# Diagonal products on TensorE for the sum of layer 0's experts, and two groups of layer 1's adaLN products at other places

## The chip, the cores and the metric

The kernel runs on one core of a Trainium2 chip. The core has five engines with a queue each: TensorE (PE; its weight loads are listed as PEld), VectorE (DVE), ScalarE (ACT), GpSimd (POOL) and SyncE (SP), which here only issues DMAs. Each engine takes its instructions in the order of its queue and waits on semaphores for the others. The metric is the device time of the kernel in microseconds, median of the runs.

## The reference

Two layers of a diffusion backbone over 512 tokens of 1024 features: 256 context tokens and 256 latent ones. Every layer computes six modulation vectors from the conditioning, mixes tokens in three branches and then sends each token to two of 16 experts:

```python
m = modulation(c, w_ada, b_ada)          # silu(c) @ w_ada + b_ada, split in 6 x 1024
mc = modulation(c_ctx, w_ada, b_ada)
h = concat(modulate(rms_norm(ctx, norm1), mc[0], mc[1]), modulate(rms_norm(x, norm1), m[0], m[1]))
mix = token_mixers(h, ...)               # neighbourhood attention, HGRN2, window attention
x = x + m[2] * mix                       # and ctx with mc
hx = modulate(rms_norm(x, norm2), m[3], m[4])
y = moe_ffn(hx, w_router, b_router, w_gate, w_up, w_down)
x = x + m[5] * y                         # and ctx with mc, in layer 0
```

In `moe_ffn` each token has two experts and two weights that sum to 1; an expert is `(silu(h @ w_gate) * (h @ w_up)) @ w_down`, and `y` is the weighted sum of a token's two rows.

## The kernel before, in words

Large products run as three passes of fp32r with the operands split into a high and a low half (`mm3`, L242 to L245). ScalarE casts the high half of a weight piece (`whi`, L231), VectorE subtracts it for the low one (`wlo`, L232). Weight pieces of 1 MB (`wraw`) come over SP's queue (L215) into a ring of slots, `wst`; in layer 0's tail it has twelve, of the tags raw, praw, mg and qraw. A slot is free when its piece has been read for the last time, by VectorE for a piece that is split, by TensorE for one that is not. SP issues in order, so a load whose slot is not free holds the later ones. A scheduler places the instructions of each queue.

**adaLN.** `ada_group(l, g)` (L252) makes 2048 columns, two of the six modulation vectors, of layer l: eight pieces of `w_ada` (L260), with each four f32 products of 32x512 that stand side by side in the array's columns (L262), 32 products in one bank, psd; then VectorE adds the bias (L266) and four DMAs on ScalarE's queue write the result to `m_dram` (L268). A product leaves two records in the trace, so a piece leaves eight. Five groups run inside layer 0's mixers, piece by piece between weight pieces of the projection (`ada_step` out of `split_piece`): (0,1), (0,2), (1,0), (1,1), (1,2). The last two hold layer 1's vectors 2 to 5, which are read first in layer 1's tail.

**Mixers.** The projection of layer 0's tokens, `psg<-hTh,whi` and its two companions, goes on between the mixers' own products. The HGRN mixer is a chain of VectorE, ScalarE, GpSimd and TensorE steps over chunks (L482 to L566) that ends in `yb`, written by VectorE at L566, and TensorE then multiplies yb by its projection.

**Router.** After the output projection each of four tiles of 128 tokens is transposed (L1098), multiplied by the router (L1106) and written to `h2d` (L1113). `route` works on two tiles at a time in small VectorE steps, TensorE counts ranks (L1273, L1274, L1283) and places tokens with one-hot masks M (VectorE L1309, TensorE L1313, 16 products for each tile). From the result come the gather indices `gix` (L1334). A branch on the largest expert count (`cnt`, L1148) follows on all engines. While this runs, `fetch` loads the first twelve pieces of expert weights into the twelve slots.

**Experts.** Each of the 16 gathers 128 rows (L1371, on GpSimd's queue), transposes them (L1402), multiplies by gate and up (4 pieces) and, one expert later, by down (2 pieces), and scatters the rows to `yd` (L1376). The pieces go out in the order in which they are used. The last two experts do not scatter: their rows stay on chip (`spare`, split in two fp32r halves) and a matrix MT carries them back to the tokens (`back_matrix`, L1447).

**Sum.** `combine` (L1636) loads the two rows y0, y1 of each token in `yd` (L1648), and for each tile of 128 tokens ScalarE scales them by the token's weights `wts` (L1654, L1655), GpSimd and VectorE add them, multiply by the modulation m5 and add to x, on 384 and 640 columns (L1656 to L1660). For the two experts on chip TensorE multiplies `spare` by MT, four products a half-tile (L1667), VectorE multiplies by m5 into `tm` (L1669) and adds to x (L1670). Tiles 0 and 1 are the context, 2 and 3 the latents; behind x follow layer 1's norm (L304, L307), the transposes (L395) and its first products, `psg<-whi,hTh`.

## Time and profile before

| | us |
|---|---|
| median of 3 runs | 1770.28 (1768.99 to 1772.41) |
| the profiled execution | 1766.91 |
| its span in the trace | 1764.8 |
| TensorE busy | 1653.8 (94%) |
| VectorE busy | 1049.4 (59%) |
| ScalarE busy | 818.7 (46%) |
| GpSimd busy | 346.2 (20%) |

The times in the rows are microseconds from the span's start. Of the 1766.91 us of the profiled execution 2.1 lie outside the span. An engine's share over the whole span does not say what limits a stage: for that the table by stretch is read, then the rows of the engine that waits there, with what ended its wait in brackets.

### The profile page before, as it was taken

Reading aid. Unit: us, or ns where it says so; the run is one execution under the profiler, and the core shown is the slowest. Engines: PE = TensorE matmul, PEld = TensorE weight load, DVE = VectorE, ACT = ScalarE, POOL = GpSimd, SP = SyncE. Lnnn points to the kernel's source line nnn. Section 1 sums busy time; section 2 is a strip of 40 time slices with the busy share of each in tenths; the row PEclk is TensorE's granted clock in tenths of the full one; section 3 lists DMA queues with packets and bytes.
Section 4 is the critical chain, followed back from the end, with each engine's and each line's share of the span. In section 5 each row is a group of like instructions: output and inputs, shape, how many; then the busy total and the mean of one; then the engine's idle time right before and its main releaser. Section 6 shows DMA issues by size and latency. Waiting matters only on the chain. (4 is left out here: it accounts for less than half of the span.)

```text
span 1764.8 us, 24182 instructions
## 1 busy us (share of the span) xinstructions
PE 1653.8 (94%) x8912; PEld 1218.6 (69%) x8913; DVE 1049.4 (59%) x1908; ACT 818.7 (46%) x1353; POOL 346.2 (20%) x343
## 2 busy tenths in 40 slices
PE   8999999999999999589999996999999999699998
PEld 4657677887677788477877774878887888443333
DVE  4328482447867335688888889488548786411101
ACT  3313232336676442368778774444446875301100
POOL 0003040222300123411221104143213202100000
PEclk9999999999999999799999997999999999899999
DMA  9895747523211355499999962322524345899996
GB/s 289 295 321 175 245 168 257 183 73 96 60 49 36 101 183 196 170 315 368 369 328 364 363 237 86 113 79 60 191 82 105 105 120 204 342 413 414 412 378 269
DMA packets 235312, 380.02 MB, mean 215 GB/s; under 512 B 33447, under 2 KB 130215, under 8 KB 225585
## 3 DMA queue, kind: packets, MB, share of 16 engines
q1 hardware_dynamic: 223248, 361.19, 59.1%
q10 hardware_dynamic: 7616, 9.43, 1.6%
q0 software_dynamic: 4320, 7.75, 1.3%
q8 instruction: 74, 1.21, 0.3%
q14 instruction: 54, 0.43, 0.1%
HBM read 370.50 MB, written 17.72 MB: 220 GB/s over the span
## 5 line engine op out<-in xcount | busy, mean ns | idle before, releaser
L232 DVE TENSOR_TENSOR wlo<-wraw,whi 128x1024 fp32r<-128x1024 f32 (+2 forms) x368 | 438.6, 1212 | 176.1 <-ACT whi L231 161.6
L231 ACT CAST whi<-wraw 128x1024 fp32r<-128x1024 f32 (+2 forms) x368 | 369.4, 1023 | 171.1 <-PE psg L245 77.2
L243 PE MATMUL psg<-hTh,whi 128*128 128x512 f32 (+1 forms) x576 | 206.6, 360 | 0.0
L244 PE MATMUL psg<-hTl,whi 128*128 128x512 f32 (+1 forms) x576 | 205.4, 357 | 0.0
L245 PE MATMUL psg<-hTh,wlo 128*128 128x512 f32 (+1 forms) x576 | 204.2, 356 | 0.0
L243 PE MATMUL psg<-whi,hTh 128*128 128x512 f32 (+1 forms) x392 | 148.6, 383 | 2.2 <-ACT hTh L373 2.1
L244 PE MATMUL psg<-wlo,hTh 128*128 128x512 f32 (+1 forms) x392 | 148.1, 379 | 0.0
L245 PE MATMUL psg<-whi,hTl 128*128 128x512 f32 (+1 forms) x392 | 147.3, 379 | 0.5 <-DVE hTl L404 0.4
L243 PEld LDWEIGHTS psg<-hTh,whi 128*128 128x128 f32 x576 | 109.1, 190 | 27.1 <-issue 10.1
L245 PEld LDWEIGHTS psg<-hTh,wlo 128*128 128x128 f32 x576 | 109.0, 190 | 19.0 <-issue 6.1
L244 PEld LDWEIGHTS psg<-hTl,whi 128*128 128x128 f32 x576 | 109.3, 190 | 16.0 <-issue 4.0
L1478 PE MATMUL psg<-wraw,xT 128*64 128x512 f32 x512 | 113.2, 595 | 2.9 <-PEq L1149 2.7
L243 PE MATMUL psg<-whi,xh 128*128 128x512 f32 x256 | 101.8, 398 | 0.7 <-ACT xh L1403 0.7
L244 PE MATMUL psg<-wlo,xh 128*128 128x512 f32 x256 | 100.0, 391 | 0.0
L245 PE MATMUL psg<-whi,xl 128*128 128x512 f32 x256 | 99.6, 390 | 0.0
L243 PEld LDWEIGHTS psg<-whi,hTh 128*128 128x128 f32 x392 | 74.3, 190 | 19.5 <-ACT hTh L373 3.8
L1478 PEld LDWEIGHTS psg<-wraw,xT 128*64 128x64 f32 x512 | 35.9, 137 | 74.4 <-issue 72.2
L245 PEld LDWEIGHTS psg<-whi,hTl 128*128 128x128 f32 x392 | 73.9, 189 | 16.8 <-DVE hTl L404 1.7
L244 PEld LDWEIGHTS psg<-wlo,hTh 128*128 128x128 f32 x392 | 74.4, 190 | 13.3 <-issue 0.5
L587 ACT ACTIVATE P<-P,smx 128x512 f32<-128x512 f32 (+1 forms) x96 | 62.2, 648 | 22.9 <-DVE smx L586 20.4
L836 POOL TENSOR_TENSOR mg<-mg,gates 128x512 f32<-128x512 f32 (+1 forms) x32 | 38.1, 1198 | 172.1 <-DVE gates L835 126.2
L1371 POOL DMA_INDIRECT xg<-h2d,gix x16 | 27.8, 1739 | 204.5 <-PE pst L1402 188.5
(414 smaller groups left out, 3256.9 us busy)
## 6 DMA issues: line engine op xcount, KB each, us to landing
wraw<-in_w_down_dram SPq DMA_DIRECT2D x64, 1024.0 KB
wraw<-in_w_ada_dram SPq DMA_DIRECT2D x40, 1024.0 KB
wraw<-in_w_in_dram SPq DMA_DIRECT2D x144, 256.0 KB
wraw<-in_w_up_dram SPq DMA_DIRECT2D x32, 1024.0 KB
wraw<-in_w_gate_dram SPq DMA_DIRECT2D x32, 1024.0 KB
wraw<-in_w_gate_dram SPq DMA_DIRECT2D x64, 512.0 KB
wraw<-in_w_up_dram SPq DMA_DIRECT2D x64, 512.0 KB
wraw<-in_w_in_dram SPq DMA_DIRECT2D x24, 1024.0 KB
```

The source lines that it names most:

```text
L231: S.copy(hi[:, :, 0:n], r[:, 2 * j:2 * j + 2, 0:n])
L232: V.tensor_tensor(lo[:, :, 0:n], r[:, 2 * j:2 * j + 2, 0:n], hi.bitcast(F32)[:, :, 0:n], ALU.subtract)
L243: PE.matmul(ps, ah, bh, start=start, stop=False)
L244: PE.matmul(ps, ah, bl, start=False, stop=False)
L245: PE.matmul(ps, al, bh, start=False, stop=stop)
L587: S.activation(flat, flat, AF.Exp, scale=-1.0, bias=m[:, 0:1], accum_out=m[:, 2:3])
L836: G.tensor_tensor(dst, dst, sg[:, i], ALU.add)
L1371: return G.indirect_dma_start(out=xg, out_offset=None, in_=h2d[l][:, :], in_offset=bass.IndirectOffsetOnAxis(ap=idx, axis=0), bounds_check ...
L1478: PE.matmul(pgu[64 * c:64 * c + 64, :], xT[:, 2 * p + k, o:o + 64], r[:, :, k, 256 * c:256 * c + 256], start=p == 0 and k == 0, stop=p == ...
```

## The change

Three things are done. Line numbers behind L253 grow by 4 to 19.

Groups (1,1) and (1,2) are no longer part of `ada_rest`. Layer 0's mixers keep three groups.

Group (1,1) goes into the router of layer 0. Its first seven pieces take the seven slots (raw, praw, mg) into which `loaded` fetched expert weights before, the eighth and four expert pieces go into the five of qraw, and one more expert piece into the first slot that falls free. The 32 products are put behind the last product of the output projection, the bias and its DMAs behind them.

Group (1,2) goes behind the experts: six pieces ahead of the loads of y rows, two behind those of tile 2, and weights of layer 1's projection come behind the loads of tile 3. Its first 24 products stand straight behind the last expert product.

`combine` now makes diagonal matrices `dg` (identity times a column of `wts`, on GpSimd, four for a pair of tiles, in the buffer of M) and lets TensorE add y0 and y1 in f32 in the same bank as the four MT products: 16 products of 128x512. ScalarE's scalings and the GpSimd and VectorE steps on y rows are gone; `tm` and the addition to x stay. The second half-tiles use a bank of the tag psg.

```diff
+    def ada_piece_of(l, g, k):
+        r = wtile([128, 4, 512])
+        loads.append(SY.dma_start(r.rearrange("p j n -> p (j n)"), A["w_ada"][l, 128 * k:128 * k + 128, 2048 * g:2048 * g + 2048]))
+        return r
+
+    def ada_group(l, g, pieces=None):
...
+            r = pieces[k] if pieces else ada_piece_of(l, g, k)
...
-        for l, g in ((0, 1), (0, 2), (1, 0), (1, 1), (1, 2)):
+        for l, g in ((0, 1), (0, 2), (1, 0)):
...
-                    fetch(len(wst))
+
+                        early.extend(ada_piece_of(1, 1, k) for k in range(len(wst)))
+                    else:
+                        fetch(len(wst))
...
-                fetch(nbuf["qraw"])
+                if full:
+                    n = 8 - len(early)
+                    early.extend(ada_piece_of(1, 1, 8 - n + k) for k in range(n))
+                    fetch(nbuf["qraw"] - n)
+                    with tc.issue_after(end.ins):
+                        deque(ada_group(1, 1, early), 0)
+                else:
+                    fetch(nbuf["qraw"])
...
+                late = [ada_piece_of(1, 2, k) for k in range(6)]
                 steps = combine(ex, x, wts, m5, xg, ys)
                 next(steps)
+                late += [ada_piece_of(1, 2, k) for k in (6, 7)]
+                next(steps)
+                deque(ada_group(1, 2, late), 0)
...
-                with tc.issue_after(after[0].ins), tc.issue_after(after[1].ins), \
-                        tc.issue_after(norms[-1].ins) if h else nullcontext():
-                    S.activation(y1[:, c0], y1[:, c0], AF.Copy, scale=wts[:, t, 1:2])
-                    S.activation(y0, y0, AF.Copy, scale=wts[:, t, 0:1])
-                    G.tensor_tensor(y0[:, c0], y0[:, c0], y1[:, c0], ALU.add)
-                    V.scalar_tensor_tensor(y0[:, c1], y1[:, c1], wts[:, t, 1:2], y0[:, c1], ALU.mult, ALU.add)
-                    for E, c in ((G, c0), (V, c1)):
-                        E.tensor_tensor(y0[:, c], y0[:, c], m5[1 - h][:, c], ALU.mult)
-                        E.tensor_tensor(x[:, t, c], x[:, t, c], y0[:, c], ALU.add)
+            dg = ex.tile([128, 2, 2, 128], F32, name="dg", tag="M")
+            for t in range(2):
+                for i in range(2):
+                    G.tensor_scalar(dg[:, t, i], ident, wts[:, 2 * h + t, i:i + 1], None, ALU.mult)
             for t in (2 * h, 2 * h + 1):
                 for c in range(2):
                     cs = slice(512 * c, 512 * c + 512)
-                    ps = ps_a()
+                    ps = ps_g() if c else ps_a()
+                    for i, y in enumerate(pairs[t]):
+                        PE.matmul(ps, dg[:, t % 2, i], y[:, cs], start=i == 0, stop=False)
                     for i, (y, _, MT) in enumerate(ys):
                         for j in range(2):
-                            PE.matmul(ps, MT[:, t], y[:, j, cs], start=i + j == 0, stop=i == len(ys) - 1 and j == 1)
+                            PE.matmul(ps, MT[:, t], y[:, j, cs], start=False, stop=i == len(ys) - 1 and j == 1)
```

TensorE's queue in the router, from the last product of the output projection (`psg<-whi,ml`) on: `C,x` are the transposes of a tile, `wrm,h2T` its router products, `ohb` the rank products, `rhs,M` the placing products, `wraw,cT` the adaLN products. First before:

```order
L245 MATMUL psg<-whi,ml 128x512
L1098 MATMUL pst<-C,x 128x128 x4
L1106 MATMUL psg<-wrm,h2T 128x16 x4
L1283 LDWEIGHTS one
L1283 MATMUL pst<-ohb,one 128x16
```

The same queue after:

```order
L245 MATMUL psg<-whi,ml 128x512
L266 MATMUL psd<-wraw,cT 32x512 x5
L1106 MATMUL pst<-C,x 128x128 x4
L266 MATMUL psd<-wraw,cT 32x512 x4
L1114 MATMUL psg<-wrm,h2T 128x16 x4
L266 MATMUL psd<-wraw,cT 32x512 x8
L1302 LDWEIGHTS one
L1302 MATMUL pst<-ohb,one 128x16
```

Twenty-eight of the 32 products stand in five groups (5, 4, 8, 8, 3) from here up to behind the first placing product, one more among the placing products of the first two tiles, and the last three behind these.

SP's queue around the branch on cnt (`TENSOR_LOAD cnt`), where `h2d` are the writes of the router's tokens. Before:

```order
L1113 DMA h2d_137<-xg_5479 128x1024
L215 DMA wraw<-in_w_up_dram 128x4x512
L215 DMA wraw<-in_w_down_dram 128x4x512
L1113 DMA h2d_137<-xg_5478 128x1024
L215 DMA wraw<-in_w_down_dram 128x4x512
L215 DMA wraw<-in_w_gate_dram 128x4x512
L215 DMA wraw<-in_w_up_dram 128x4x512
L1148 TENSOR_LOAD cnt
```

After:

```order
L1121 DMA h2d_137<-xg_5361 128x1024
L215 DMA wraw<-in_w_gate_dram 128x4x512
L254 DMA wraw<-in_w_ada_dram 128x2048
L1121 DMA h2d_137<-xg_5360 128x1024
L215 DMA wraw<-in_w_gate_dram 128x4x512
L215 DMA wraw<-in_w_up_dram 128x4x512
L215 DMA wraw<-in_w_gate_dram 128x4x512
L215 DMA wraw<-in_w_up_dram 128x4x512
L1163 TENSOR_LOAD cnt
```

Ahead of these rows SP issued seven expert pieces before and issues seven of w_ada now. Behind the branch it now asks for seven expert pieces whose slots are free by then (up, gate, up, down, down, gate, up).

TensorE's queue behind the last expert product (`psg<-whi,al`), where `C,xn` are the transposes of layer 1 and `hTh` its first products. Before:

```order
L245 MATMUL psg<-whi,al 128x512
L1667 MATMUL psa<-spare,MT 128x512 x19
L395 MATMUL pst<-C,xn 128x128 x2
L1667 MATMUL psa<-spare,MT 128x512
L395 MATMUL pst<-C,xn 128x128 x6
L243 MATMUL psg<-whi,hTh 128x512
```

After:

```order
L245 MATMUL psg<-whi,al 128x512
L266 MATMUL psd<-wraw,cT 32x512 x24
L1683 MATMUL psa<-y_9643,dg 128x512
L1683 MATMUL psg<-y_9643,dg 128x512
L1683 MATMUL psa<-y_9644,dg 128x512
L1686 MATMUL psa<-spare,MT 128x512 x4
L1683 MATMUL psg<-y_9644,dg 128x512
L1686 MATMUL psg<-spare,MT 128x512 x4
```

The rows for tiles 1 to 3 follow in the same manner, with the other eight adaLN products in tile 2 and some transposes of the context between tiles; all 16 dg and all 32 MT products now stand ahead of the first layer-1 product. Before, four MT products stood ahead of the last expert products and eight behind the first 32 products of layer 1.

## Rows read from the trace of the kernel before

**Rows 1.** The page: busy time and share by engine, and the 40 slices.

```profile
PE 1653.8 (94%) x8912; PEld 1218.6 (69%) x8913; DVE 1049.4 (59%) x1908; ACT 818.7 (46%) x1353; POOL 346.2 (20%) x343
...
PE   8999999999999999589999996999999999699998
```

**Rows 2.** Stretches: bounds, length, busy PE PEld DVE ACT POOL, clock, DMA share, GB/s.

```profile
192.60:310.00 117.40, 114.40 (x626) 82.21 (x625) 59.17 (x100) 32.87 (x58) 20.67 (x30) 0.99 0.67 226
222.00:256.00 34.00, 33.49 (x216) 24.51 (x209) 31.88 (x58) 11.32 (x17) 16.18 (x24) 1.00 0.45 151
721.80:753.10 31.30, 8.31 (x92) 6.79 (x91) 25.31 (x103) 5.59 (x11) 8.64 (x7) 0.57 0.64 212
...
797.00:1017.00 220.00, 210.70 (x996) 172.55 (x995) 190.83 (x187) 175.50 (x212) 45.15 (x31) 1.00 1.00 359
1061.30:1084.40 23.10, 9.85 (x28) 5.35 (x26) 22.19 (x26) 11.57 (x18) 14.90 (x12) 0.63 0.28 91
1084.40:1115.60 31.20, 29.80 (x131) 22.61 (x130) 23.44 (x42) 15.61 (x31) 5.77 (x5) 0.95 0.25 80
```

**Rows 3.** Stretches again, busy PE and PEld of the adaLN products (L262) alone.

```profile
192.60:219.40 26.80, 6.85 (x48) 1.19 (x48) 0.94 0.82 268
219.40:283.10 63.70, 11.98 (x72) 2.12 (x72) 1.00 0.45 154
283.10:300.00 16.90, 1.17 (x12) 0.16 (x8) 1.00 1.05 344
```

**Rows 4.** PE in time: start, length, instruction, [idle before <-what ended it]; mixers.

```profile
205.12 1.06 PE L262 MATMUL psd<-wraw,cT 128*32 128x512 f32 x8 [1.02 <-DMA wraw<-in_w_ada_dram]
207.45 1.93 PE L262 MATMUL psd<-wraw,cT 128*32 128x512 f32 x8 [1.26 <-DMA wraw<-in_w_ada_dram]
...
260.66 1.05 PE L262 MATMUL psd<-wraw,cT 128*32 128x512 f32 x2
...
280.42 2.78 PE L262 MATMUL psd<-wraw,cT 128*32 128x512 f32 x24
283.14 0.50 PE L243 MATMUL psg<-yb,whi 128*128 128x512 f32 x1
```

**Rows 5.** DVE in time: the last write of yb.

```profile
270.52 0.69 DVE L566 TENSOR_TENSOR yb<-pst,yb 128x512 fp32r<-128x512 f32 x1 [1.19 <-ACT yb L565]
```

**Rows 6.** PE in time, in the router and at the first expert.

```profile
723.78 0.63 PE L1098 MATMUL pst<-C,x 128*128 128x128 f32 x4 [1.60 <-DVE v L1252]
...
730.89 0.22 PE L1283 MATMUL pst<-ohb,one 128*128 128x16 bf16 x2 [4.42 <-DVE ohb L1267]
...
734.20 0.23 PE L1313 MATMUL psa<-rhs,M 128*128 128x3 bf16 x1 [3.00 <-DVE M L1309]
...
741.69 0.17 PE L1274 MATMUL psa<-ohb,utr 128*128 128x16 bf16 x1 [3.06 <-DVE ohb L1267]
...
753.11 1.94 PE L1402 MATMUL pst<-C,xg 128*128 128x128 f32 x8 [5.20 <-DMA xg<-h2d,gix]
```

**Rows 7.** DVE and ACT in time, in the router and at the first expert.

```profile
735.92 0.69 DVE L1309 TENSOR_TENSOR M<-iot,rnb 128x1024 bf16<-128x1024 bf16 x1 [0.71 <-PE psa L1313]
...
754.36 1.32 ACT L1403 CAST xh<-pst 128x512 fp32r<-128x512 f32 x2 [25.07 <-PE pst L1402]
```

**Rows 8.** Waits from 753 to 1061: who for whom, total, times, longest.

```profile
POOL xg L1371 <- PE pst L1402: 188.5, 14, 18.8
```

**Rows 9.** PE and DVE in time, behind the experts.

```profile
1075.41 3.35 PE L1667 MATMUL psa<-spare,MT 128*128 128x512 f32 x7 [7.39 <-DVE tm L1669]
...
1084.43 0.79 PE L243 MATMUL psg<-whi,hTh 128*128 128x512 f32 x1
...
1092.92 1.08 PE L1667 MATMUL psa<-spare,MT 128*128 128x512 f32 x4
...
1075.88 1.28 DVE L1670 TENSOR_TENSOR x<-x,tm 128x512 f32<-128x512 f32 x2
```

**Rows 10.** PE in time, the f32 products of layer 1's experts.

```profile
1564.12 3.70 PE L1512 MATMUL psa<-y,WT 128*128 128x512 f32 x8
```

**Rows 11.** POOL in time, the four masks of `back_matrix`.

```profile
911.64 2.86 POOL L1452 TENSOR_SCALAR M<-C,rnk 128x128 f32<-128x128 f32 x4 [7.67 <-PE pst L1454]
```

More of the change, by code (lines that the diff above doesn't have):

```diff
@@ L244, in mm3 @@
         PE.matmul(ps, ah, bl, start=False, stop=False)
[L245 removed]
+        return PE.matmul(ps, al, bh, start=False, stop=stop)
     m_dram = [tc.dram_tile([2, 6 * D], F32, name=f"m_dram{l}") for l in range(2)]
@@ L938, in output_projection @@
                             sl = slice(128 * t, 128 * t + 128)
-                            mm3(ps[t], mh[:, 4 * hh + k, sl], ml[:, 4 * hh + k, sl],
+                            end = mm3(ps[t], mh[:, 4 * hh + k, sl], ml[:, 4 * hh + k, sl],
                                 w[hh][0][:, k], w[hh][1][:, k], hh == 0 and k == 0, hh == 1 and k == 3)
@@ L948, in output_projection @@
                                 tile_done(t)
+        return end
     class Ahead:
@@ L1049, in tail @@
                 blg = rp.tile([128, len(rr), 16], F32, name="blg")
-                lgs, placed = [None], None
+                lgs, placed, early = [None], None, []
                 def vectors(last):
@@ L1137, in tail @@
                 with tc.tile_pool(name=f"wo{l}", bufs=1, side=other) as op:
-                    output_projection(l, op, mg, x, vectors, loaded, tile_done)
+                    end = output_projection(l, op, mg, x, vectors, loaded, tile_done)
                 if not full:
@@ L1446, in back_matrix @@
     def back_matrix(ex, e, nt, rnk, comb):
-        M = ex.tile([128, nt, 128], F32, name="M")
+        M = ex.tile([128, nt, 128], F32, name="M", tag="M")
         pt = ps_t((128, nt, 128))
```

24 lines of the change are left out of this document (10 added, 14 removed).

## The prediction

> **What bounds the kernel now.** I read the page first, then one view for each of the three stretches that the change touches. TensorE is busy for 1653.8 us of 1764.8, 94% of the span [rows 1], so only its own time, or a place where it waits, can move the end. The row of 40 slices shows where it waits: slices of 9 nearly everywhere, a 5 and a 6 in the middle of the span [rows 1]. The table by stretch puts numbers to that [rows 2]. From 192.6 to 310 us, in layer 0's mixers, TensorE works 114.40 of 117.40 us: what is taken out there is gain, if nothing else comes late. From 721.8 to 753.1, the router, it works 8.31 of 31.30 and VectorE 25.31: a chain of small VectorE steps sets the time. From 797 to 1017, the experts, it works 210.70 of 220.00 while the DMA engines are busy for a share of 1.00. From 1061.3 to 1084.4, layer 0's sum, it works 9.85 of 23.10 and VectorE 22.19: here the adding of expert rows sets the time, and TensorE's next work, layer 1's projection, begins at 1084.43 [rows 9].
>
> The change takes 64 adaLN products (two groups of 32, 16 pieces of weights) out of the first stretch and puts 32 into the second and 32 into the fourth, where it also lets TensorE do the adding.
>
> **Part A, the mixers: what goes.** All adaLN products from 192.92 us on belong to the two groups. Their busy time stands in three rows: 6.85 us up to 219.4, 11.98 up to 283.1, 1.17 after that, together 20.0 [rows 3]. Busy time counts a product's tail under the next one: a group of 24 records shows 2.78 but the next product starts 2.72 after it [rows 4]. Summed by starts, which is what TensorE gains, the 16 groups give 19.2. Two of them also wait for their weights, 1.02 and 1.26 us, and after the second wait the granted clock is down, so that 8 records take 1.93 in place of 1.06 [rows 4]; about 0.9 of that is in the 19.2, some 0.6 lies in the next three products. All together at most 19.2 + 2.3 + 0.6 = 22.1.
>
> Not all need be gained. The HGRN mixer is a chain through VectorE, which from 222 to 256 is busy 31.88 of 34.00 [rows 2]. Its last result, yb, is written from 270.52 for 0.69, so until 271.2 [rows 5]; TensorE begins the products on it at 283.14 [rows 4], 11.9 us later. If that chain did not move at all, TensorE would gain these 11.9 and the 1.0 of the last group behind it: 12.9. But the chain starts behind the projection that ends at 219.4, and 6.85 + 2.3 + 0.6, some 9.7 us, of what goes lies ahead of it. So yb is ready at about 261.5, and TensorE, relieved of 21.1 us by then, would come to it at about 262. The two just meet. I take 20.5 gained, bounds 12.9 and 22.1.
>
> **Part B, the router: 32 products come in.** TensorE's own rows there say what room there is: it idles 1.60 us before the last transposes, 4.42 before the rank products, 3.00 before the first placing product, 3.06 before the second pair of tiles, and 5.20 for the gathered rows [rows 6]. The order shows groups of 5, 4, 8, 8, 3, 1 and 3 products in these places. Four products (8 records) take 1.06 at full clock and 1.93 at the lower one; one alone (2 records) takes 1.05 [rows 4], as much as four, which lie side by side in the array. The granted clock of this stretch is 0.57 [rows 2], between its two levels. The 5 (about 2 us) fill the 1.60 and run over by 0.3; the 4 stand where TensorE waits for VectorE's copies, and add as much; the first 8 (2 to 3.9) fit in the 4.42; the next 8 stand in the 3.00 and may run over by 0.4; the 3 and the 1 stand between placing products, 1 to 1.9 each, with little room; the last 3 have the 3.06. Behind the 3 and the 1 VectorE waits: its third mask M stood for 0.71 on TensorE already [rows 7], and the router steps of the second pair of tiles are queued behind it. The bias sum of the group, one VectorE step over 512 columns, such as the mask's 0.69 [rows 7], now stands in those steps and waits for the last product. I sum 0.3 + 0.3 + 0.4 + 0.7 + 0.8 = 2.5 later (the 5, the 4, the second 8, the 3 and the 1, the bias sum); bounds -1 (all in the waits, and a clock that stays up shortens the rest) and +4.5 (every group at the lower clock). ScalarE's DMAs of the group replace casts there, and ScalarE idled 25.07 us before the first expert's cast at 754.36 [rows 7], so they cost nothing unless the branch on cnt comes late.
>
> [...]
>
> **Part C, the experts: less weight on hand.** Eight of the twelve slots first hold adaLN weights and one of these is filled again, so 5 pieces of expert weights in place of 12 are loaded when the branch is passed, and seven are asked for at once behind it. An expert takes 18.8 us (the longest of 14 waits of the gather queue for the transposes of xg, one whole turn [rows 8]) and 6 pieces, so 3.13 us each. At 359 GB/s, the rate of 797 to 1017 [rows 2], seven pieces of 1.05 MB land in 20.4 us, the first after about 3. The sixth piece is wanted 15.6 us into the experts, the twelfth 34.4, each some 4 earlier for its split. So there are 8 to 10 us to spare at either end, and the lead need not grow back: the DMA engines carry what the experts use. I price C at 0. If that cover were gone, for instance if the seven landed side by side at 20, the sixth would be some 9 us late; that is its upper bound.
>
> **Part D, the sum on TensorE, and 32 more products.** What goes: ScalarE's scalings, GpSimd's and most of VectorE's row steps, behind which TensorE waits 7.39 us at one place [rows 9]. What comes, all between the last expert product (1061.1) and layer 1's first: 32 adaLN products in 8 groups of 0.9, 7.3 us; 16 f32 products of 128x512, for which the nearest row is a group of 8 records, 4 products, in 3.70 us [rows 10], so 0.92 each, 14.8; the 32 products of the last two experts, 4 in 1.08 by their row and 0.23 by their starts [rows 9], 7.4, of which 8 lay behind layer 1's first product before. Sum 29.5, so TensorE's first layer-1 product goes from 1084.4 to about 1092. Against that it finds a full clock (before, the stretch had 0.63 [rows 2], and the first such product took 0.79 us [rows 9]), no more 8 products in between, and the transposes done: before, the first 96 products of layer 1 took from 1084.4 to 1115.6, with TensorE busy 29.80 at 0.95 [rows 2]; now 96 at 0.23 and the transposes left, some 25, end at about 1117.5. GpSimd makes four diagonal matrices for each half; the row of four such operations is 2.86 us [rows 11], the second four wait until the first are read, and the third tile's first product for them: some 0.5 to 1. D is +2.5: bounds -2 and +7, the first if the clock holds and nothing waits, the second if each tile waits 1 to 2 us for its matrices, rows or norm. VectorE is no bound: it keeps a product and an addition for each half-tile, two of the latter in 1.28 [rows 9].
>
> **Sum.** -20.5 + 2.5 + 0 + 2.5 = -15.5. Against the profiled run's own 1766.9 that is 1751.4; the median of the three runs shown is 1770.3, 3.4 above it, so 1754.8.
>
> **Rivals.**
> 1. The HGRN chain becomes the bound: TensorE gains only 12.9 in the mixers. For it: VectorE's 31.88 of 34.00. Against: the chain starts 9.7 us sooner. Total -8, 1762. Chance 0.12.
> 2. The sum is limited by its own order: each tile's products stand behind transposes that wait for the norm of an earlier tile, D is +9. For it: TensorE takes its work in one order only, and the norm has ScalarE, VectorE and GpSimd steps. Total -9, 1761. Chance 0.12.
> 3. Slower: the clock between 1061 and 1092 falls to the lower level and stays. One wait of 1.0 and one of 1.3 us did it at 207 [rows 4], and the same stretch had 0.63 [rows 2]. The 29.5 us are then 59 at worst; at 0.63 they are 46.8, 17.3 more, total +2, 1772; at the lower level throughout +14, 1784. It decides where the mean granted clock of these 29.5 us is under 0.66 (29.5 / 0.66 is 15.2 more). Against it: the 24 products ahead have their weights early and run without a gap. Chance 0.07.
> 4. The clock in the router stays up, B is -1: total -19, 1751. Chance 0.08. The number rests on the bound in B.
> 5. Rivals 1 and 2 together, or the change moves work without gain elsewhere: about -1.5, 1769. Chance 0.04.
>
> **How the numbers follow.** My forecast has 0.57. The range must hold 8 in 10: from 1747 (A -22, B -1, D 0) to 1767, which takes in rivals 1, 2 and 4 and the upper bounds of B and D one at a time. Within 0.2%, 3.5 us, is about what cannot be told from no change. Faster: 0.57 + 0.12 + 0.12 + 0.08, less a little for the tails, 0.87; same 0.06; slower 0.07.
>
> **What would show it.** No adaLN row after 192 us in the mixers, and the products on yb starting near 262 with no wait for VectorE; the first expert's transposes some 18 us before 753; no TensorE wait for weights in the experts; the diagonal products in groups between about 1047 and 1076 at a clock of 1.0; the first layer-1 product some 31 us behind the last expert product, where it was 23. A wait for yb of over 3 us makes rival 1, a granted clock under 0.8 behind the experts rival 3.

## The result, and the profile after

The changed kernel takes 1761.9 us, the median of five runs from 1758.8 to 1765.9. The kernel before takes 1771.1 in runs beside it (1769.0 to 1772.4). The ratio is 0.9944, with an interval from 0.9923 to 0.9965. That is 9.2 us less, where the prediction had 15.5 less and 1755. The time lies inside the range, and the gain is real but three fifths of the forecast.

The profiled execution took 1758.8 us with a span of 1757.0; that of the kernel before took 1766.9 with 1764.8. The page of the kernel after, as in [rows 1]:

```profile
PE 1662.5 (95%) x8944; PEld 1223.9 (70%) x8945; DVE 1036.0 (59%) x1896; ACT 812.6 (46%) x1345; POOL 335.6 (19%) x339
...
PE   8999999999999999599999999999999999699998
```

TensorE has 32 instructions more and is busy 8.7 us longer; VectorE, ScalarE and GpSimd are each busy less. Of the two dips in the middle of [rows 1] one is left, the router's 5. The table by stretch answers to [rows 2]; its columns are the same.

```profile
192.60:222.00 29.40, 28.81 (x146) 24.37 (x145) 22.20 (x33) 10.39 (x14) 5.25 (x6) 1.00 0.34 105
222.00:256.00 34.00, 31.98 (x211) 27.19 (x210) 27.79 (x50) 13.02 (x28) 14.79 (x23) 1.00 0.24 78
...
700.80:739.50 38.70, 19.06 (x156) 8.53 (x155) 27.31 (x105) 8.46 (x13) 8.73 (x7) 0.68 0.72 254
730.50:739.50 9.00, 0.14 (x3) 0.07 (x2) 5.81 (x13) 0.00 (x0) 3.15 (x2) 0.50 0.81 288
787.00:1007.00 220.00, 210.78 (x987) 172.70 (x986) 190.12 (x188) 174.50 (x211) 49.59 (x35) 0.99 1.00 361
1050.00:1081.00 31.00, 30.99 (x146) 15.31 (x146) 16.66 (x30) 8.52 (x17) 4.33 (x6) 1.00 0.42 140
```

Three things stand here. In the mixers TensorE idles 2.0 of the 34 us from 222 on, where [rows 2] have 0.5. In the last 9 us before the first expert (730.5 to 739.5) TensorE does nothing while the DMA engines are at 0.81. Behind the experts (1050 to 1081) TensorE works 30.99 of 31.00 us at full clock, where [rows 2] have 9.85 of 23.10 at 0.63.

To say where the 9.2 us came from, the span is cut at rows that both kernels have. The stages below are differences between starts of such rows, in us. *Mixers*: from layer 1's first adaLN transposes to the first product on yb. *Projection*: to the last product of the output projection. *Router*: to the last placing product. *Gather*: to the first expert's transposes of xg. *Experts*: to the last expert product. *Sum*: to ScalarE's fourth copy of vv in layer 1. The last column is the span. Kernels of the experiments stand in the same table; "again" is a second profile of the same kernel.

| kernel | mixers | projection | router | gather | experts | sum | span |
|---|---|---|---|---|---|---|---|
| before | 93.9 | 438.6 | 25.9 | 5.4 | 307.8 | 54.8 | 1764.8 |
| before again (e6) | 90.5 | 442.2 | 26.1 | 5.2 | 310.1 | 54.8 | 1769.7 |
| after | 74.5 | 436.6 | 29.7 | 9.1 | 310.2 | 57.1 | 1757.0 |
| after again (e11) | 74.5 | 440.2 | 30.3 | 9.0 | 310.8 | 56.8 | 1764.1 |
| sum alone (e2) | 91.4 | 439.6 | 26.1 | 5.6 | 310.4 | 47.1 | 1760.1 |
| products left out (e7) | 73.6 | 436.8 | 25.9 | 4.8 | 310.9 | 47.1 | 1739.0 |
| one group back (e1) | 89.3 | 440.3 | 26.2 | 5.5 | 310.2 | 52.8 | 1767.4 |
| the same again (e9) | 86.1 | 436.6 | 26.2 | 4.7 | 307.9 | 52.8 | 1752.4 |
| other group back (e8) | 88.3 | 440.2 | 30.4 | 5.3 | 311.2 | 49.1 | 1766.3 |
| the same again (e10) | 87.7 | 438.8 | 29.8 | 5.6 | 310.1 | 49.1 | 1760.3 |
| loads behind gather (e3) | 74.5 | 441.2 | 27.2 | 5.2 | 311.2 | 58.3 | 1757.1 |
| last pieces late (e4) | 74.5 | 441.2 | 25.9 | 7.4 | 312.7 | 57.1 | 1761.1 |
| both (e5) | 74.5 | 439.2 | 25.6 | 6.4 | 308.3 | 58.0 | 1752.6 |
| rows ahead (e12) | 74.5 | 437.3 | 25.9 | 6.8 | 309.3 | 62.2 | 1756.5 |

The change touches neither the projection nor most of the experts, and these two columns still move by 5 us from one execution to the next. So one profile of each kernel says where time went only in the other columns. There the change gains 16 to 19 us in the mixers, and loses 3.6 to 4.4 in the router, 3.6 to 3.9 at the gather and 2.0 to 2.3 in the sum.

**The mixers, after.** TensorE and VectorE in time around yb, as in [rows 4, 5]:

```profile
264.00 0.39 PE L245 MATMUL psg<-hTh,wlo 128*128 128x512 f32 x1
264.23 0.39 PE L243 MATMUL psg<-yb,whi 128*128 128x512 f32 x1
...
260.71 0.69 DVE L570 TENSOR_TENSOR yb<-pst,yb 128x512 fp32r<-128x512 f32 x1 [1.35 <-ACT yb L569]
```

yb is written until 261.4 and TensorE comes to it at 264.2 with no wait. The prediction had 261.5 and 262: TensorE is 2.2 us later than that, and earlier in the stage it waits 3.0 us for results of the chain (Q and ob), which the table under e9 to e11 counts.

**The router and the gather, after.** TensorE, VectorE, GpSimd and SP in time, as in [rows 6, 7]; the third number is how long, in brackets the idle time before:

```profile
716.92 1.92 PE L266 MATMUL psd<-wraw,cT 128*32 128x512 f32 x2
718.77 1.07 PE L1332 MATMUL psa<-rhs,M 128*128 128x3 bf16 x15
719.77 1.93 PE L266 MATMUL psd<-wraw,cT 128*32 128x512 f32 x6
...
739.52 1.94 PE L1421 MATMUL pst<-C,xg 128*128 128x128 f32 x8 [8.88 <-DMA xg<-h2d,gix]
...
721.75 0.69 DVE L270 TENSOR_TENSOR mr<-mr,psd 128x512 f32<-128x512 f32 x1 [1.60 <-PE psd L266]
...
730.48 1.28 POOL L1390 DMA_INDIRECT xg<-h2d,gix  x1 [19.19 <-SPq L1164]
...
730.73 0.39 SPq L215 DMA_DIRECT2D wraw<-in_w_up_dram  x1
731.22 0.44 SPq L215 DMA_DIRECT2D wraw<-in_w_gate_dram  x1
```

The wait for the gathered rows is 8.88 us; it was 5.20 [rows 6]. GpSimd asks for the rows at 730.48, and from 730.73 on SP asks for the expert pieces that it had held back, 1 MB each. Before the change GpSimd asked at 747.73 and SP for its next piece only at 752.54; between 747.7 and 753.1 the DMA engines stood at a share of 0.50.

**The sum, after.** TensorE in time behind the last expert product, which before had the wait of 7.39 us [rows 9]:

```profile
1050.01 5.36 PE L266 MATMUL psd<-wraw,cT 128*32 128x512 f32 x48
1055.30 1.12 PE L1683 MATMUL psa<-y,dg 128*128 128x512 f32 x2
1056.26 1.02 PE L1683 MATMUL psg<-y,dg 128*128 128x512 f32 x2
...
1060.70 1.88 PE L1683 MATMUL psa<-y,dg 128*128 128x512 f32 x4
1062.01 1.50 PE L1686 MATMUL psa<-spare,MT 128*128 128x512 f32 x4
...
1080.96 0.39 PE L243 MATMUL psg<-whi,hTh 128*128 128x512 f32 x1
```

The products follow each other without a gap. By their starts a diagonal product takes some 0.9 us (1055.30 to 1056.26), and an MT product the 0.23 that the prediction took. Layer 1's first product starts 31.3 us behind the last expert product and takes 0.39.

### The profile page after: what moved, and what is told of

It reads as the page before. It is cut to its first block, busy times and chain, and to the rows that moved or that the text cites. A ratio compares the mean times of both kernels' runs of the same rounds, so it can differ in the third digit from the quotient of the medians.

```text
span 1757.0 us, 24218 instructions
## 1 busy us (share of the span) xinstructions
PE 1662.5 (95%) x8944; PEld 1223.9 (70%) x8945; DVE 1036.0 (59%) x1896; ACT 812.6 (46%) x1345; POOL 335.6 (19%) x339
## 5 line engine op out<-in xcount | busy, mean ns | idle before, releaser
L232 DVE TENSOR_TENSOR wlo<-wraw,whi 128x1024 fp32r<-128x1024 f32 (+2 forms) x368 | 441.2, 1218 | 181.7 <-ACT whi L231 171.0
L243 PEld LDWEIGHTS psg<-whi,hTh 128*128 128x128 f32 x392 | 74.0, 189 | 19.4 <-ACT hTh L377 3.8
L591 ACT ACTIVATE P<-P,smx 128x512 f32<-128x512 f32 (+1 forms) x96 | 62.1, 648 | 22.1 <-DVE smx L590 19.6
```

The costliest lines, as they stand in the source:

```text
L232: V.tensor_tensor(lo[:, :, 0:n], r[:, 2 * j:2 * j + 2, 0:n], hi.bitcast(F32)[:, :, 0:n], ALU.subtract)
L243: PE.matmul(ps, ah, bh, start=start, stop=False)
L591: S.activation(flat, flat, AF.Exp, scale=-1.0, bias=m[:, 0:1], accum_out=m[:, 2:3])
```

## Experiments

The theory after the comparison: the mixers gave what was forecast, the router cost a little more, and the gather is late because the expert pieces asked for behind the branch share the DMA engines with it. The rivals: that the gain is the sum's and not the moved products'; that the HGRN chain bounds the mixers after all; that the experts, with less weight on hand, are slower.

**One group back (e1).** Group (1,1) returns to the mixers; group (1,2) and the sum stay as changed.

```diff
-        for l, g in ((0, 1), (0, 2), (1, 0)):
+        for l, g in ((0, 1), (0, 2), (1, 0), (1, 1)):
...
-                        early.extend(ada_piece_of(1, 1, k) for k in range(len(wst)))
+                        fetch(len(wst))
...
-                        deque(ada_group(1, 1, early), 0)
+                fetch(nbuf["qraw"])
```

> Group (1,1) goes back into the mixers, so the router and the expert loads are those of before; group (1,2) behind the experts and the diagonal products stay. My theory (in the changed kernel the mixers gave 21.0 us back, the router took 3.7, the first gather 3.7 and the first expert's lower clock 1.2 of it, the sum 2.3): mixers about -10.5 against before, router and first gather as before (31.3 us from the last product of the output projection to the first expert's transposes), sum +2.3, in all some -8, within 2 us of the changed kernel. Rival, the working of the prediction (router +2.5, loads and gather at nothing): 8 us slower than the changed kernel, about -2 against before.

Measured: 1762.0 us (1757.5 to 1769.2, six runs; the profiled one is the longest) beside 1771.9, ratio 0.9939 [0.9923, 0.9955]. Router and gather are as before the change (26.2 and 5.5), so their losses come from this group. But the time is that of the full change: the mixers gained little, 89.3, where 10.5 less than before was expected. The sum missed too, the other way: 52.8 in place of some 57, with the same 32 adaLN products as the changed kernel. In this order of the queue five of them and two diagonal products stand ahead of the last expert product, where the changed kernel has none:

```profile
1049.07 1.90 PE L266 MATMUL psd<-wraw,cT 128*32 128x512 f32 x10
```

**The sum alone (e2).** All five groups are in the mixers; only the diagonal products are left of the change.

```diff
-        for l, g in ((0, 1), (0, 2), (1, 0)):
+        for l, g in ((0, 1), (0, 2), (1, 0), (1, 1), (1, 2)):
...
-                late = [ada_piece_of(1, 2, k) for k in range(6)]
...
-                deque(ada_group(1, 2, late), 0)
```

> All five adaLN groups stay in the mixers; only the sum by diagonal products is done. My theory: TensorE comes to layer 1's first product about as long after the last expert product as before (16 x 0.92 + 32 x 0.23 and transposes, some 23.7 us against 23.3), but at full clock and with no MT products behind, which gave 5.3 us back in the changed kernel: about -5 against before. Rival: without the 24 adaLN products in front the first diagonal products wait for the rows or the second four matrices, the clock is at its lower level again, and nothing is gained: 0.

Measured: 1761.9 us (1759.1 to 1763.6), ratio 0.9941 [0.9925, 0.9957]. This is as good as the whole change, and twice the 5 us that were expected. The sum's stage falls from 54.8 to 47.1, 7.7 us, although GpSimd's matrices are waited for once:

```profile
1071.50 1.98 PE L1673 MATMUL psa<-xg,dg 128*128 128x512 f32 x4 [1.04 <-POOL dg L1667]
```

So the two ideas of the change must be told apart: the diagonal products give the time, and moving 64 products gives, as it was done, nothing that these intervals (some 3 to 4 us to either side) can tell from zero. From e2 to after the table shows -16.9 in the mixers, +3.6 in the router, +3.5 at the gather and +10.0 in the sum: +0.2 together. Part of the 10.0 is a shift across the cut: e2 has four diagonal and two MT products ahead of the last expert product, in place of waits of 1.46 and 0.45 us that after has there.

**Loads behind the gather (e3).** After the branch a small DMA that reads the first gathered row is queued on SP, and the experts' loads are issued behind it. As a side effect four expert pieces are loaded ahead of the branch instead of five, and the group's products lie a little differently in the router.

```diff
                 past_slots(lambda: overflow(l, side, nt, cap, rnk, rhs, cnt))
+                held = tc.dram_tile([1, 16], F32, name="held")
+                hold = SY.dma_start(held, xg[0][0:1, 0:16])
+                held_ = ExitStack()
+                held_.enter_context(tc.issue_after(hold.ins))
...
+                held_.close()
```

> The changed kernel with a small copy on SP's queue, behind the branch, that reads the first gathered rows; the eight expert pieces behind the branch are issued after it. My theory: the first gather is late (8.88 us of waiting where before had 5.20) because these loads share the DMA engines with it; the wait goes back to 5 to 5.5, the time falls by 3.5, and TensorE still waits for no weights in the experts. Rival: the gather is late for the pieces issued ahead of the branch, or for its own issue; then the wait stays at 8 to 9 and the time stays, or grows as the loads come 5 us later.

Measured: 1756.3 us (1752.8 to 1760.5), ratio 0.9913 [0.9896, 0.9931]. The wait is back at its old length. TensorE and SP in time, and the stretch of the wait:

```profile
737.66 1.94 PE L1426 MATMUL pst<-C,xg 128*128 128x128 f32 x8 [5.00 <-DMA xg<-h2d,gix]
...
737.54 0.32 SPq L1202 DMA_DIRECT2D held<-xg  x1
737.97 0.40 SPq L215 DMA_DIRECT2D wraw<-in_w_gate_dram  x1
```

```profile
732.00:738.00 6.00, 1.00 (x13) 0.94 (x13) 4.69 (x13) 0.00 (x0) 3.18 (x2) 0.50 0.47 132
```

The DMA share is 0.47 where it was 0.81, and the wait 5.00 where it was 8.88. SP asks for the expert pieces 5.5 us behind the first gather (732.49), where in after it is 0.25. In the experts, with still less weight on hand, TensorE waits for no piece. So the late gather comes from the loads that are asked for with it, and the lead is not needed. The times of e3 and of the changed kernel lie 5.6 us apart; by the table the gather gives 3.9 and the router, whose products lie differently here, 2.5, and the sum takes 1.2 back.

**Last pieces late (e4).** Five of the eight pieces of group (1,1) are multiplied where the change has them; the other three, 12 products, are put behind the last placing product, into the wait for the gather.

```diff
+                    steps11 = ada_group(1, 1, early)
...
-                        deque(ada_group(1, 1, early), 0)
+                        for _ in range(5):
+                            next(steps11)
+                    with tc.issue_after(last_place[0].ins):
+                        deque(steps11, 0)
```

> The changed kernel with the last three pieces of group (1,1), 12 products, and with them the bias sum, behind the last placing product, in TensorE's wait for the gathered rows. My theory: the lone groups of 3, 1 and 3 products and VectorE's wait of 1.60 us for the bias sum are what makes the router 3.7 us longer; from the last product of the output projection to the last row of placing products it goes from 28.8 us to about 25.5, and the time falls by 3 against the changed kernel, the first gather staying late. Rival: the router is longer because its VectorE steps are, with other work in their way; then it stays near 28.8 and the time stays.

Measured: 1759.6 us (1757.3 to 1763.2), ratio 0.9929 [0.9915, 0.9944]. The router takes 25.9, as before the change: the last 12 products and the bias sum were its whole loss, and the 20 products that stay cost nothing that this column shows. The gather, which was expected to stay late, lands 5.2 us after it is asked for, since SP asks for its first piece only 7.7 us behind it. But TensorE waits for ScalarE: 2.35 us at the branch, ahead of the first transposes, and 1.14 for the cast ahead of the first product. ScalarE's four DMAs of the group's result, which need the bias sum, stand in its queue ahead of that cast (in e5 they start behind its first half). PE and ACT in time:

```profile
741.55 1.47 PE L1427 MATMUL pst<-C,xg 128*128 128x128 f32 x8 [2.35 <-ACTq L1168]
744.16 0.80 PE L243 MATMUL psg<-whi,xh 128*128 128x512 f32 x1 [1.14 <-ACT xh L1428]
...
740.00 2.73 ACTq L272 DMA_DIRECT2D m_dram<-mr  x4
```

**Both (e5).** The edits of e3 and e4 together.

> The loads behind the gather and the last three adaLN pieces behind the placing products, together. My theory: the router up to the last placing product is as long as before (26 us from the last product of the output projection), the first gather's wait ends as before, and only the price in the sum is left: 1755, some 1 to 2 us better than with the loads behind the gather alone (there the router kept 1.2). Rival: the 12 products in the wait for the gathered rows end after them and hold the first expert; then it is 2 to 3 us slower than with the loads alone.

Measured: 1753.3 us (1751.8 to 1755.8) beside 1769.4, ratio 0.9908 [0.9893, 0.9924]. That is 16 us, the forecast's gain, and the best version of this study. TensorE in time, and two stretches:

```profile
730.29 4.93 PE L266 MATMUL psd<-wraw,cT 128*32 128x512 f32 x18
735.52 1.06 PE L266 MATMUL psd<-wraw,cT 128*32 128x512 f32 x6 [0.30 <-PEq L1168]
736.51 1.09 PE L1432 MATMUL pst<-C,xg 128*128 128x128 f32 x8
737.96 0.50 PE L243 MATMUL psg<-whi,xh 128*128 128x512 f32 x1 [0.36 <-ACT xh L1433]
738.30 0.40 PE L244 MATMUL psg<-wlo,xh 128*128 128x512 f32 x1
```

```profile
730.20:736.50 6.30, 6.00 (x27) 1.19 (x26) 3.52 (x11) 0.00 (x0) 3.15 (x2) 0.64 0.47 139
736.50:744.50 8.00, 7.64 (x39) 5.99 (x37) 7.08 (x8) 4.74 (x6) 1.44 (x1) 1.00 0.97 330
```

The products fill the gather's wait, and at its end TensorE is at the full clock: the first expert's transposes take 1.09 us where they took 1.94, and its products 0.40 where e3's row at the same place, behind an idle wait, has 0.63. In e5 the granted clock has a mean of 0.64 over the 6.3 us that these products fill and 1.00 over the 8 us behind them. In e3 it is 0.50 over the 6 us that hold the idle wait, and in after 0.61 over the first 8 us of the experts.

**Before again (e6).** A second profile of the unchanged kernel, as a measure of what differs without a cause in the program.

> The kernel before once more, for a second profile. My theory: the profiled execution of before was a good one; the changed kernel and its four variants all take 2.4 us or more longer in layer 0's experts and 1.8 us longer at one place of layer 1's experts, where nothing was changed, because the granted clock falls there for some microseconds in some executions. Then this profile has a fall at one of these places too, and the experts near 310 us (first transposes to last product) or layer 1's sixth pair at 30.9 in place of 29.2. Rival: the change costs it; then this profile reads 307.8 and 29.2 again.

Measured: 1771.9 us, span 1769.7. The experts take 310.1, as in after, and the mixers 90.5 in place of 93.9: one of the waits for w_ada that [rows 4] show is gone, the other is shorter, and the 8 records behind it take 1.07 us, where the first profile had 1.93.

```profile
205.38 1.06 PE L262 MATMUL psd<-wraw,cT 128*32 128x512 f32 x8
206.83 1.07 PE L262 MATMUL psd<-wraw,cT 128*32 128x512 f32 x8 [0.39 <-DMA wraw<-in_w_ada_dram]
```

So about 3.4 us of what the mixers took in the first profile, and the 2.4 us that the experts seemed to lose, belong to the one execution that was profiled.

**Products left out (e7).** The 64 products, their weights and their sums are not computed; the two groups hold the bias alone. The twelve slots load expert weights as before; the rest is as in after. The run measures what the products cost in their new places.

> The changed kernel with the 64 products of groups (1,1) and (1,2), their weights and their sums left out: layer 1's vectors 2 to 5 are the bias alone, and the twelve slots load expert weights as before. My theory: mixers -21, router and gather as before, sum -7.7 as in the run of the sum alone, in all 28 us under before, 1743; so the new places of the 64 products cost 18 to 19 us, nearly what they cost in the mixers. Rival, the prediction: the new places cost little over half of that, and this kernel lies only 10 us under the changed one.

Measured: 1739.8 us (1738.8 to 1745.2) beside 1769.4, ratio 0.9839 [0.9820, 0.9858]. Between its span and after's lie 18.0 us: 3.8 in the router, 4.3 at the gather, 10.0 in the sum. TensorE's own time for the 64 is about 15 at full clock (32 take 7.3 by their starts behind the experts). So in sum the waits into which they were put hid nothing of it: 20 of them are free in the router (e4), but the loads make the gather late. In e5, 13.5 us above this kernel, the 64 cost a little less than their own time.

**The other group back (e8).** Group (1,2) returns to the mixers, (1,1) stays in the router.

```diff
-        for l, g in ((0, 1), (0, 2), (1, 0)):
+        for l, g in ((0, 1), (0, 2), (1, 0), (1, 2)):
...
-                deque(ada_group(1, 2, late), 0)
```

> Group (1,2) goes back into the mixers, (1,1) stays in the router, the diagonal products stay. The one group left runs where the first of the two ran, ahead of the HGRN chain. My theory: the mixers then gain only some 4 to 8 us, since the chain through VectorE starts as late as before, the router and the gather cost 7.4, the sum gives 7.7: 4 to 8 us under before, 1764 to 1767, slower than the changed kernel. Rival: each group is worth its own 10 us wherever it stands; then -10.5 + 7.4 - 7.7, some 1761, as the changed kernel.

Measured: 1763.3 us (1759.6 to 1768.4), ratio 0.9962 [0.9948, 0.9976]. The router's loss is there (30.4), but the gather's is not (5.3), though (1,1) holds the same slots until the same products. The gather was expected to be late. In this kernel SP asks for the pieces 2.1 us behind the first gather (753.03 and 750.95), and the DMA share in the wait is 0.53: the time between the two requests decides, as in e3. The second gather of the same execution shows it too: it is asked for 0.5 us ahead of the pieces and lands after 9.1 us, the first after 5.2. GpSimd in time, and from the view of xg the shorter, the median and the longer landing of the two:

```profile
750.95 1.28 POOL L1387 DMA_INDIRECT xg<-h2d,gix  x1 [19.90 <-DVE six L1353]
752.53 1.90 POOL L1387 DMA_INDIRECT xg<-h2d,gix  x1 [0.30 <-POOLq L1164]
...
DMA to landing us min/median/max: 5.2/7.2/9.1
```

In every profile here in which SP asks 2 us or more behind the first gather, that gather lands after 4.6 to 5.4 us; in the two of after, where SP asks 0.25 and 0.08 us behind it, after 8.9 and 8.8. The mixers gained as little as in e1: 88.3.

**Second profiles (e9, e10, e11)** of e1, e8 and the changed kernel, one execution each.

> The kernel with group (1,1) back in the mixers once more, for a second profile: the first fell on the longest of its six runs (1769.2 us, median 1762.0) and there the mixers gained 2.9 us only. My theory: with one group left ahead of the HGRN chain TensorE waits in the chain (a wait of 2.5 us for GpSimd's Q, five others) and the gain from the start of layer 1's first adaLN transposes to the end of the output projection stays under 8 us in any execution. Rival: the first profile was disturbed by late adaLN weights, and the gain is 10 to 11.

> The kernel with group (1,2) back in the mixers once more: as for the other group, under 8 us by my theory (4.0 in the first profile), 10 to 11 by the rival.

> The changed kernel once more, for a second profile. My theory: the first gather is waited for 8 to 9.5 us again, the router is again 3.5 to 4 us longer up to its last placing product than in before, and the experts, 310.2 us in the first profile, may read 308 to 311, as in the two profiles of before. Rival: the gather's wait was an accident of the first execution and reads 5.

Measured: 1754.3, 1762.4 and 1766.1 us. The router at 30, the gather at 9 and the mixers at 74.5 in after, at 86 to 89 with one group in them, repeat. By its own measure, up to the end of the output projection, e9 missed: mixers and projection take 522.7, 9.8 to 10 less than in the two profiles of before, not under 8 less; e10 gains 6.0 to 6.2. The mixers alone give 4.4 to 7.8 in e9, and the rest lies in the projection, which the edit does not touch. The mixers are the odd case: with five groups they take 90.5 to 93.9, with four 86 to 89, with three 74.5. The reason stands in e9's rows of TensorE and VectorE:

```profile
253.29 1.56 PE L529 MATMUL psa<-Q,K 128*128 128x256 f32 x6 [2.46 <-POOL Q L543]
...
269.08 0.69 DVE L570 TENSOR_TENSOR yb<-pst,yb 128x512 fp32r<-128x512 f32 x1 [1.35 <-ACT yb L569]
```

The table splits the mixers' stage by TensorE's rows: time by starts of the adaLN products, and all waits. (The stage is counted here from the first of the transposes, 0.3 us sooner.)

| kernel | stage | adaLN products | waits | of these for Q, ob, bk |
|---|---|---|---|---|
| before again | 90.8 | 17.3 | 1.1 | 0.2 |
| sum alone | 91.7 | 17.3 | 2.0 | 0.2 |
| one group back again | 86.5 | 7.6 | 6.7 | 6.0 |
| other group back again | 88.0 | 7.6 | 6.3 | 6.0 |
| after | 74.8 | 0 | 3.5 | 3.0 |

The first group taken out gives 9.7 us of products and turns some 6 of them into waits for the HGRN chain. The second gives 7.6 more, and with it 3 us of the waits go away again. The last write of yb says why. Counted from the stage's start it ends at 78.9 to 82.3 us with all groups (before, e6, e2), at 79.3 to 82.5 with one out (e1, e9, e8, e10), and at 72.0 with both. With one out, the products of the other stand at the same places as the first ones of before, from 4 to some 30 us behind the start, so the chain does not move at all; only what lay beside it is gone.

**Rows ahead (e12).** e5, with the loads of the expert rows ahead of group (1,2)'s pieces in SP's queue and its products behind the second tile's first diagonal products. In after TensorE waits 1.46 and 0.45 us in the last expert for its split rows, which e2 fills with diagonal products.

```diff
-                late = [ada_piece_of(1, 2, k) for k in range(6)]
                 steps = combine(ex, x, wts, m5, xg, ys)
                 next(steps)
-                late += [ada_piece_of(1, 2, k) for k in (6, 7)]
+                late = [ada_piece_of(1, 2, k) for k in range(8)]
                 next(steps)
-                deque(ada_group(1, 2, late), 0)
+                with tc.issue_after(first_sum[0].ins):
+                    deque(ada_group(1, 2, late), 0)
...
```

> As e5_both, and the loads of the expert rows of the first three tiles stand ahead of the eight weight pieces of group (1,2) in SP's queue, the group's products behind the first tile's diagonal products. In the profile of the changed kernel TensorE waits 1.46 us at 1043.56 and 0.45 at 1045.21 for the split of the last expert's hidden rows, while in e2_sum_alone diagonal products stand in that place. Theory: there the rows come before the adaLN weights, so the diagonal products can fill these waits; here one of them moves ahead of the last expert products, so the wait before them is some 1 us shorter, and experts plus sum take 338 to 339 us where e5_both took 339.4 (308.3 + 31.2 less a rounding). Time within 0.1% of e5_both, ratio to before 0.990. Rival: the pieces asked for later come too late. Eight of 1.05 MB at 361 GB/s, the rate of the experts, take 23 us; if the first products of the group wait for them, TensorE shows waits for wraw of 2 to 5 us between the diagonal products, and the time is 1755 to 1758.

Measured: 1758.4 us (1753.4 to 1758.7) beside 1770.1, ratio 0.9925 [0.9907, 0.9943], not better than e5. The 1.46 us wait stands as it was; the diagonal product came to lie behind it. And no piece of w_ada is waited for. The price shows elsewhere: the sum's stage takes 62.2 in place of 58.0. Layer 1's first pieces are asked for at 1068.86, where e5 has 1055.40. In SP's queue they now stand behind a store of the sum (`xd<-x`), ahead of which SP waited 19.6 us for x, and TensorE's first product of layer 1 waits 2.35 us for its split. Whether their slots would have been free sooner is not shown. TensorE and SP in time, and SP's wait:

```profile
1038.23 0.50 PE L243 MATMUL psg<-whi,ah 128*128 128x512 f32 x1 [1.46 <-ACT ah L1454]
1039.27 1.02 PE L1694 MATMUL psa<-y,dg 128*128 128x512 f32 x2
...
1078.35 0.73 PE L243 MATMUL psg<-whi,hTh 128*128 128x512 f32 x2 [2.35 <-ACT whi L231]
...
1068.43 0.32 SPq L1704 DMA_DIRECT2D xd<-x  x1
1068.86 2.04 SPq L215 DMA_DIRECT2D wraw<-in_w_in_dram  x3
...
SPq L1704 <- DVE x L1702: 19.6, 1, 19.6
```

Both the theory and the rival of this run fell: the queue behind the moved loads, not the loads themselves, set the end of this stage.

## Why the prediction was nearly right

**Part A, the mixers (-20.5).** The mechanism held: no wait for yb, which is written at the time foreseen. The term was 1 to 4.5 us too large, about 3 against the middle of the profiles. It counted 2.3 us of waits for weights and 0.6 behind them that the profile of before showed; a second profile of before shows 0.4, and e2, with the same five groups, 1.2. And it left out the waits of 3.0 us for Q and ob, of which before again has 0.2. Three executions with all groups in the mixers take 93.9, 90.5 and 91.4; six without the two take 74.5. The gain is 16 to 19.4. Rival 1, the HGRN chain as the bound, falls for the whole change and holds for half of it: with one group out, TensorE waits 6 us for that chain. That some 9.7 us of what goes lie ahead of the chain was right for the whole: yb came 9.8 us sooner. Not foreseen was that either half alone would not move the chain, since the group that stays keeps those places.

**Part B, the router (+2.5).** It cost +3.6 to +4.4, inside the bound of 4.5. e4, in which the last 12 products and the bias sum are taken away, has the router at 25.9, so they are the whole loss: among them the lone product (1.92), the last three (1.93) and the bias sum, for which VectorE waited 1.60. The prediction had named the lone product and the bias sum, at 1.5 together with the three before them, and put the last three at nothing; the lone one and the last three ran at a granted clock of 0.50, as in before the 8 records of 1.93 in the mixers, where those of 1.06 and the 24 products behind the experts had 1.00. The groups of 5 and 4, at 0.3 each, cost nothing that e4 shows. Rival 4, a clock that stays up, was the author's estimate and falls: the stretch from 700.8 has a mean of 0.68, and the first expert's transposes still ran at 0.50, in 1.94 us.

**Part C, the experts' lead (0).** This is the step that failed, though not in the way its bound had it. The lead did not matter: no piece is waited for, in after as in e3 with less of it. Of the prediction's sentence that seven pieces are "asked for at once behind" the branch the consequence was missed: the gather is asked for at the same place, and its few rows then share the DMA engines with these pieces (busy for a share of 0.81 in the wait, against 0.50 before and 0.47 in e3). That is +3.6 to +3.9 us, in both profiles of after, and gone in e3. The prediction had the seven pieces landing side by side as the way to a loss; it weighed that only for the sixth piece, 15 us later, and not for the first transfer that TensorE waits for. How far apart the two requests lie decides: 0.25 us in after, 0.08 in its second profile, 2.1 in e8, where nothing was lost. What sets that distance no run isolates.

**Part D, the sum (+2.5).** The stage went from 54.8 to 57.1, +2.3. First layer-1 product at 31.3 us behind the last expert product against "some 31", and a clock of 1.00. Rivals 2 and 3 fall: TensorE waits 0.01 us there. But the single number hid two large ones. The term had 7.3 for the adaLN products, which leaves -4.8 for the rest; the diagonal products gained 7.7 (e2), and the adaLN products beside them cost 10.0. The two errors cancel, so that the term came out is in part luck. The 10.0 is no fixed price either: in e1 and e9, with group (1,1) back, the same 32 products cost 5.7 over e2 (52.8), and in e8 and e10, without them, the stage is at 49.1.

**The sum.** Against the forecast of -15.5, A gave about 3 less, B took 1.2 more and C 3.7: -7.6, to be held against -9.2 between the medians. The two spans differ by -7.8, but that this is so near is chance: in this pair of profiles the mixers gave 19.4, and stages that the change hardly touches (projection -2.0, experts +2.4, the ends of the span +1.5) moved as well. That spans and medians differ is within what single executions differ by. e5 undoes C and most of B and lands at -16. Rival 5, a change without gain, falls for the whole, but e2 shows that it describes the moved products in the form that they have here.

## What to carry to other kernels

Before work is put into a wait, ask whether it brings something along that shares the wait's cause: here the wait for a gather went from 5.20 to 8.88 us with the loads that the moved pieces had pushed behind the branch, and with these asked for 5.5 us behind the gather it was 5.00, and TensorE waited for no piece (e3). Split a change of two ideas before its sum is believed: one gave nearly all the time, the other gave 17 us in one place and lost 17 in three. Read any wait of which the sum makes a term from a second profile of the same kernel, because a 1 us wait for a DMA, and the clock behind it, may be that execution's alone: here 1.26 us, with 1.93 for the products behind it, became 0.39 and 1.07 (e6).

## What the runs showed of the hardware

**Thirteen of the sixteen experts take 18.70 to 18.79 us each, in all four profiles of this table.** Cut at the first product of each expert, the table gives the first expert, the next seven, the ninth (in which GpSimd's masks for the last two are made), the six behind it, and the last with its end, in us:

| kernel | first | next seven | ninth | next six | last |
|---|---|---|---|---|---|
| before | 13.55 | 18.75 to 18.78 | 22.28 | 18.74 to 18.76 | 26.23 |
| before again | 14.69 | 18.74 to 18.79 | 23.49 | 18.74 to 18.78 | 26.20 |
| after | 14.80 | 18.75 to 18.79 | 23.46 | 18.72 to 18.79 | 26.14 |
| both (e5) | 13.05 | 18.73 to 18.78 | 24.12 | 18.70 | 26.07 |

Only the first and the ninth differ by more than 0.2 us, and there by over 1. In the ninth the granted clock behind one short wait differs. Before the change, TensorE in time and two stretches of 4 us:

```profile
912.80 0.33 PE L1454 MATMUL pst<-C,M 128*128 128x128 f32 x1 [1.34 <-POOL M L1452]
```

```profile
912.00:916.00 4.00, 2.71 (x20) 2.21 (x20) 1.83 (x4) 1.65 (x4) 2.50 (x4) 1.00 1.04 392
916.00:920.00 4.00, 4.00 (x19) 3.16 (x18) 2.14 (x4) 2.07 (x4) 0.00 (x0) 1.00 0.91 319
```

And after:

```profile
900.49 0.33 PE L1473 MATMUL pst<-C,M 128*128 128x128 f32 x1 [1.33 <-POOL M L1471]
```

```profile
900.00:904.00 4.00, 3.09 (x20) 2.63 (x20) 1.83 (x3) 1.37 (x3) 3.33 (x5) 0.85 1.05 393
904.00:908.00 4.00, 4.00 (x15) 3.15 (x14) 1.41 (x3) 1.46 (x3) 2.25 (x4) 0.73 1.04 387
```

Around the same wait, 1.34 and 1.33 us in the same place of the program, the granted clock is 1.00 in both stretches of one execution and 0.85 and 0.73 in those of the other, where the ninth takes 23.46 us in place of 22.28. The ninth of before again, the same program as before, is as long as that of after. The projection's column moves as well, from 436.6 to 442.2 us, though no edit touches it; its mean granted clock, worked out from the traces, is 0.996 in before (438.6 us) and in after (436.6). What made it longer in other profiles is not shown. So columns of one kernel move by some 4 us from one execution to the next, and a difference of that size in one profile is no effect of a change.

**In the mixers 9.7 us less TensorE work was not 9.7 us less time, for the HGRN chain stood close.** With one group out the mixers gave 1 to 8 us for 9.7 us of products, with both 16 to 19 for 17.3 of them: the chain's last write stayed where it was with one out, and came 7 to 10 us sooner with both.
